# S5 token gather and scatter through a DRAM scratch, and the HGRN2 gates' affine steps on ScalarE

## The chip, the cores and the metric

The kernel runs on one core of a Trainium2 chip. The metric is the device time of one execution in microseconds; of several executions the median counts. TensorE is written PE, VectorE DVE, ScalarE ACT, GpSimd POOL, and SyncE, which issues most DMAs, SP.

## What is computed

A decoder trunk of two layers over one sequence of 512 tokens and 1024 channels, in float32. Layer 0 splits one input projection `z = h @ ev_w_in` into five parts of 512 channels. The first goes through S5, a diagonal complex state space in 32 groups of 16 channels and 64 states; the four others are query, forget gate, value and output gate of HGRN2 with four heads of 128:

```
y = gelu(s5(u));  y_a = y * sigmoid(y @ w_glu + b_glu)
forget = lb + (1 - lb) * sigmoid(f_pre)
key    = (1 - lb) * sigmoid(-f_pre)
query  = silu(q_raw)
o = chunk_gated_linear(query, key, i_raw, log(forget))
y_b = rms_norm(o, norm_g) * silu(g_raw)
x = x + gate * (concat(y_a, y_b) @ ev_w_out)
```

A SwiGLU feed-forward follows, then layer 1 (GLA mixer and feed-forward) and a last norm. Each sub-layer's shift, scale and gate (adaLN) come from `cond @ ada_w`, six pieces of 1024 columns a layer.

## The kernel before, in words

Activations lie with channels on partitions and the 512 tokens in the free dimension. Each float32 weight and activation is split in a high and a low part (`whi`, `wlo`; `hhi`, `hlo`), and a projection takes three matmuls for each pair of blocks (`proj`, L275 to L277, 128x512; `proj_tok`, L299 to L301, 128x256).

The stage that the change touches is the mixer of layer 0. Its four projections per head are named hq (query), hf (forget), hv (value) and hg (output gate). They are written in this order: S5 block 0, `hg_fq(0)`, S5 block 1, values of heads 0 and 1, `hg_fq(1)`, S5 block 2, their output gates, the cores of heads 0 and 1, S5 block 3, values of heads 2 and 3, `hg_fq(2)`, outputs of heads 0 and 1, gelu, `hg_fq(3)`, gates, the S5 gate (`s5_glu`), the cores of heads 2 and 3, and the output projection. This is not the order that runs: the Tile framework's scheduler orders the instructions of each engine from their dependences and a simulated timeline, so a change in one step moves others.

`s5_block` handles 128 channels. Its input projection lies in PSUM as uT, 128 channels by 512 tokens. It wants four tokens side by side: U has partition 32 r + c, for r the place in a group of four tokens and c a channel of 32. So 16 copies of 32x128 (L775) move a piece each across partitions and gather every fourth token. Two sets of matmuls (vps, with the weights Wn made from wnp) bring U to the states; VectorE and POOL rotate them (tiles rz..a to d), two scans of VectorE (L792) run the recurrence over 128 groups, and the matmuls yp add the direct term (Kz) and the states' output (Wd0z, Wd1z). Then 16 ScalarE copies of 32x128 bring yp back to channels by tokens (`yf`). POOL makes block q + 1's tables (B..a, B..b, W..a, W..b) in the meantime.

`hg_fq` projects, takes sigmoids on ScalarE, and does query, key K and gate lg on VectorE, the last two as affine steps (`tsv`, a tensor_scalar, L111 and L113). The core of a head takes products of K and of e (query times decay) with running totals (tot) at seven levels of distance 1, 2, 4 to 64; at each, VectorE makes the products, PE the scores (`lv`, L465) and VectorE writes them under a mask into `sc`. kht, st, S and o_h follow: transposed keys, state sums, states, and outputs. y_h is the head's normalised output, yT its transpose, dgp the first step of heads 2 and 3.

The adaLN weights come in tiles `ar`, which SP loads into two buffers a size; VectorE sums them into `acc` with the condition as scalar (`ada_run`, L202 and L204), and a piece ends in four matmuls (`fold`, L210). acc02 and fold02 are the pieces 2 and 4 of layer 0, acc03 and fold03 the piece 3. Weight loads advance this chain (`ada_steps`), which keeps program order.

Of the kernel before, what the change touches and what calls it, by code (L numbers as in the profile page):

```python
# [8 lines left out]
F32 = mybir.dt.float32  # L9
# [8 lines left out]
P = 128  # L18
# [23 lines left out]
def trunk(  # L42
# [11 lines left out]

    cp = ctx.enter_context(tc.tile_pool(name="cp", bufs=1))
    wp = ctx.enter_context(tc.tile_pool(name="wp", bufs=3))
    xp = ctx.enter_context(tc.tile_pool(name="xp", bufs=1))
    hp = ctx.enter_context(tc.tile_pool(name="hp", bufs=2))
    tp = ctx.enter_context(tc.tile_pool(name="tp", bufs=1))
# [25 lines left out]
    def act(o, i, f, **kw):  # L85
        return A.activation(out=o, in_=i, func=f, **kw)  # L86
# [19 lines left out]
    def ttv(e, o, a, b, op):  # L106
        e.tensor_tensor(out=o, in0=a, in1=b, op=op)  # L107
# [147 lines left out]
        ada_steps()  # L255
        return w

    def split(e, src, name, th, tl):
        hi = tt(f"hi_{name}", th, dtype=F32R)
        lo = tt(f"lo_{name}", tl, dtype=F32R)  # L260
        act(hi, src, AF.Copy)
        ttv(e, lo, src, hi.bitcast(F32), ALU.subtract)
        return hi, lo

    def blocks(w, cols=slice(0, P)):
# [480 lines left out]
    def s5_tables(q):  # L746
# [15 lines left out]
        tact(ph, ph, AF.Sin, scale=TWO_PI)  # L762
        return cosT, ph

    def s5_block(q, uT, mats, rot):

        rho = prm[3]
        Km, Wn, (Wr, Wi) = mats
        cosT, sinT = rot
        shp = [P, 4, P]  # L770
        U = tt(f"U{q}", "X" if q < 3 else "s", (P, 4, P))
        for j in range(4):
            for s in range(4):
                r = 3 - s
                V.tensor_copy(out=U[32 * r : 32 * r + 32, j, :], in_=uT[32 * j : 32 * j + 32, s:T:4])  # L775
        vps = []
        for i in range(2):
            ps = ps_b(f"vps{q}{i}", (P, 4, P))
# [24 lines left out]
        for j in range(4):  # L803
            PE.matmul(yp[:, j, :], lhsT=Km[:, j].rearrange("p t c -> p (t c)"), rhs=U[:, j, :], start=True, stop=False)
            PE.matmul(yp[:, j, 1:], lhsT=Wr[:, j, :], rhs=t[0][:, j, 0 : P - 1], start=False, stop=False)
            PE.matmul(yp[:, j, 1:], lhsT=Wi[:, j, :], rhs=z[0][:, j, 0 : P - 1], start=False, stop=True)
        yf = tt(f"yf{q}", "r")
        for j in range(4):
            for s in range(4):
                act(yf[32 * j : 32 * j + 32, s:T:4], yp[32 * s : 32 * s + 32, j, :], AF.Copy)  # L810
        return yf

    def s5_glu(yf):
        wg = []
        for i in range(2):
            w = wsplit(wraw(s5_w_glu[0, i * 2 * P : (i + 1) * 2 * P, :], 2, f"wg{i}", T), 2, f"wg{i}", T, V)
            wg += [tuple(z[:, k, :] for z in w) for k in range(2)]
        yr = [split(V, y, f"yr{k}", "s", "s") for k, y in enumerate(yf)]
        res = []
        for m in range(4):  # L820
            ps = mm_ps(f"glu{m}")
            proj(ps, [tuple(z[:, m * P : (m + 1) * P] for z in w) for w in wg], yr)
            y = tt(f"ys{m}", "s")
            tact(y, ps, AF.Sigmoid, bias=cols2[:, 12 + m : 13 + m])
            ttv(G, y, y, yf[m], ALU.mult)
            res.append(split(V, y, f"ys{m}", "s", "s"))
        return res

# [190 lines left out]
    def hg_fq(hd):  # L1019
        c0 = S5W + hd * P  # L1020
        hi, lo = wload(win[:, c0 : c0 + P], KT, f"hq{hd}")
        psq = mm_ps(f"hq{hd}")
        proj(psq, blocks((hi, lo)), h)
        c0 = S5W + 512 + hd * P
        hi, lo = wload(win[:, c0 : c0 + P], KT, f"hf{hd}")
        ps = (ps_a if hd < 2 else mm_ps)(f"hf{hd}")
        proj(ps, blocks((hi, lo)), h)
        Q = tt(f"hq{hd}", "t")
        K = tt(f"hk{hd}", "t")
        lg = tt(f"lg{hd}", "t")  # L1030
        tact(Q, psq, AF.Sigmoid)
        tact(lg, ps, AF.Sigmoid)
        tact(K, ps, AF.Sigmoid, scale=-1.0)
        ttv(V, Q, Q, psq, ALU.mult)
        tsv(V, K, K, oml[:, hd : hd + 1], ALU.mult)
        tsv(V, lg, lg, oml[:, hd : hd + 1], ALU.mult, lb[:, hd : hd + 1], ALU.add)
        return Q, K, lg

    def hg_v(pr):
# [216 lines left out]
```

## Time and profile before

| | us |
|---|---|
| runs | 1358.05, 1355.7, 1357.15 |
| median | 1357.15 |
| the profiled execution's own time | 1364.62 |
| its span | 1362.8 |
| start of its first output-projection matmul | 295.7 |
| PE busy | 1286.2 (94%) |
| DVE busy | 797.2 (58%) |
| ACT busy | 487.5 (36%) |
| POOL busy | 151.0 (11%) |

The span is the time from the first to the last recorded instruction of the execution, and its own time is what the device counted for it; the mean granted PE clock was 0.967 of full speed. Busy time is the union of an engine's instructions, DMA issues left out. Matmuls are pipelined: a record is longer than the pitch from one to the next, so a dense stretch is counted by starts. A bracket at the end of a timeline row gives the idle time before the instruction and what ended it.

### The profile page before, as it was taken

The page shows a single profiled execution, that of the slowest core. Times are in us where ns is not written, and L with a number is a line of the kernel's source. Part 1 is how long each engine was busy: PE and PEld are TensorE (multiplying, and loading weights), DVE is VectorE, ACT ScalarE, POOL GpSimd, SP SyncE. Part 2 cuts the span into 40 slices and gives each one's busy share as a digit, 9 for nine tenths or more (in the row PEclk, how much of TensorE's full clock was granted, in tenths as well). Part 3 has the DMA queues.
Part 4 walks back from the last instruction along what each step waited for, and adds up shares of the span by engine and source line. Part 5 has one row for each costly group of instructions (what it writes and reads, how often), then busy time and mean ns, then how long its engine had stood idle before and what let it go on. Part 6 is the DMA issues. An engine that isn't in the chain of part 4 may idle for free.

```text
span 1362.8 us, 18262 instructions
## 1 busy us (share of the span) xinstructions
PE 1286.2 (94%) x6949; PEld 1103.4 (81%) x6949; DVE 797.2 (58%) x1511; ACT 487.5 (36%) x851; POOL 151.0 (11%) x148
## 2 busy tenths in 40 slices
PE   6598899799899999999999999999899999999997
PEld 3377887778888888888889999998788888888886
DVE  4979796887865566665445446557653333333344
ACT  5253556423532322222334434432442322232232
POOL 1764451120100000000000000000100000000000
PEclk9779998889899999999999999999999999999999
DMA  8624540534067768987333232213223323433222
GB/s 293 163 63 129 150 140 16 126 94 132 18 142 188 202 174 213 214 219 198 106 106 94 65 92 63 74 49 97 62 82 104 93 74 103 117 93 93 79 86 83
DMA packets 222824, 159.69 MB, mean 117 GB/s; under 512 B 16752, under 2 KB 195248, under 8 KB 222736
## 3 DMA queue, kind: packets, MB, share of 16 engines
q1 hardware_dynamic: 221696, 157.48, 42.2%
q10 hardware_dynamic: 1040, 1.05, 0.3%
q8 instruction: 54, 0.88, 0.3%
q14 instruction: 34, 0.28, 0.1%
HBM read 156.40 MB, written 2.10 MB: 116 GB/s over the span
## 4 chain that ended last, share of the span: by engine, by line
PE 78%; DVE 12%; DMA 4%; ACT 2%; issue 2%; POOL 1%; SPq 0%; DVEq 0%; ACTq 0%
PE f L275 18%; PE f L276 18%; PE f L277 18%; DMA ar<-in_ada_w_dram 3%; PE op L276 2%; PE op L275 2%; PE op L277 2%; PE lv_g L465 2%; DVE acc L204 2%; PE gr L300 1%; PE gr L301 1%; PE gr L299 1%; PE gv L301 1%; PE gv L300 1%; PE gv L299 1%
## 5 line engine op out<-in xcount | busy, mean ns | idle before, releaser
L276 PE MATMUL f<-hlo_f,whi_f 128*128 128x512 f32 (+1 forms) x736 | 281.5, 383 | 0.2 <-DVE hlo_f L116 0.2
L275 PE MATMUL f<-hhi_f,whi_f 128*128 128x512 f32 (+1 forms) x736 | 280.9, 384 | 0.5 <-ACT hhi_f L86 0.5
L277 PE MATMUL f<-hhi_f,wlo_f 128*128 128x512 f32 (+1 forms) x736 | 280.8, 382 | 0.0
L86 ACT ACTIVATE whi_f<-raw_f 128x1024 fp32r<-128x1024 f32 x88 | 93.3, 1061 | 307.0 <-PE f L276 169.3
L107 DVE TENSOR_TENSOR wlo_f<-raw_f,whi_f 128x1024 fp32r<-128x1024 f32 x88 | 107.7, 1224 | 115.1 <-ACT whi_f L86 114.8
L276 PEld LDWEIGHTS f<-hlo_f,whi_f 128*128 128x128 f32 x736 | 140.1, 190 | 27.0 <-DVE hlo_f L116 0.8
L275 PEld LDWEIGHTS f<-hhi_f,whi_f 128*128 128x128 f32 x736 | 139.8, 191 | 27.0 <-ACT hhi_f L86 1.0
L277 PEld LDWEIGHTS f<-hhi_f,wlo_f 128*128 128x128 f32 x736 | 140.1, 191 | 26.5
L204 DVE SCALAR_TENSOR_TENSOR acc<-ar,cond,acc 128x512 f32<-128x512 f32 x154 | 120.1, 780 | 41.6 <-DMA ar<-in_ada_w_dram 40.0
L277 PE MATMUL f<-hi_g,wlo_c 128*128 128x512 f32 x312 | 121.7, 390 | 0.0
L276 PE MATMUL f<-lo_g,whi_c 128*128 128x512 f32 x312 | 121.6, 390 | 0.0
L275 PE MATMUL f<-hi_g,whi_c 128*128 128x512 f32 x312 | 121.2, 390 | 0.0
L86 ACT ACTIVATE whi_c<-raw_c 128x768 fp32r<-128x768 f32 (+1 forms) x56 | 44.9, 801 | 161.8 <-PE f L276 114.1
L107 DVE TENSOR_TENSOR g<-g,f 128x512 f32<-128x512 f32 x44 | 30.3, 688 | 109.3 <-PE f L277 109.3
L107 DVE TENSOR_TENSOR wlo_c<-raw_c,whi_c 128x768 fp32r<-128x768 f32 (+1 forms) x56 | 50.3, 898 | 57.6 <-ACT whi_c L86 57.5
L276 PEld LDWEIGHTS f<-lo_g,whi_c 128*128 128x128 f32 x312 | 58.6, 188 | 12.1
L275 PEld LDWEIGHTS f<-hi_g,whi_c 128*128 128x128 f32 x312 | 58.6, 188 | 12.1
L277 PEld LDWEIGHTS f<-hi_g,wlo_c 128*128 128x128 f32 x312 | 58.6, 188 | 12.1
L116 DVE SCALAR_TENSOR_TENSOR x<-f,mod,x 128x512 f32<-128x512 f32 (+1 forms) x36 | 24.8, 689 | 39.4 <-PE f L277 39.2
L107 POOL TENSOR_TENSOR na_m<-na_m,nsq_m 128x256 f32<-128x256 f32 x7 | 5.7, 818 | 365.3 <-DMA raw_c<-in_ffn_w_dram 337.9
L300 PE MATMUL gv<-wlo_gv,hhi_m 128*128 128x256 f32 x128 | 36.7, 287 | 0.0
L301 PE MATMUL gv<-whi_gv,hlo_m 128*128 128x256 f32 x128 | 36.6, 286 | 0.0
(667 smaller groups left out, 2677.9 us busy)
## 6 DMA issues: line engine op xcount, KB each, us to landing
raw_f<-in_ffn_w_dram SPq DMA_DIRECT2D x88, 512.0 KB, 3.8
ar<-in_ada_w_dram SPq DMA_DIRECT2D x256, 128.0 KB, 3.7
ar<-in_ada_w_dram SPq DMA_DIRECT2D x64, 256.0 KB, 5.3
raw_c<-in_ffn_w_dram SPq DMA_DIRECT2D x32, 384.0 KB, 3.5
raw_c<-in_ffn_w_dram SPq DMA_DIRECT2D x24, 320.0 KB, 3.2
raw_gv<-in_od_w_in_dram SPq DMA_DIRECT2D x8, 512.0 KB, 4.4
raw_gr<-in_od_w_in_dram SPq DMA_DIRECT2D x8, 512.0 KB, 4.0
raw_o<-in_ev_w_out_dram SPq DMA_DIRECT2D x8, 384.0 KB, 3.4
```

The lines of the kernel that those rows point to most:

```text
L86: return A.activation(out=o, in_=i, func=f, **kw)
L107: e.tensor_tensor(out=o, in0=a, in1=b, op=op)
L116: V.scalar_tensor_tensor(out=o, in0=a, scalar=s, in1=b, op0=op0, op1=op1)
L204: ins = V.scalar_tensor_tensor(out=acc, in0=w, scalar=c_, in1=acc, op0=ALU.mult, op1=ALU.add)
L275: PE.matmul(ps, lhsT=hi, rhs=ah[:, ts], start=(i == 0), stop=False)
L276: PE.matmul(ps, lhsT=hi, rhs=al[:, ts], start=False, stop=False)
L277: ins = PE.matmul(ps, lhsT=lo, rhs=ah[:, ts], start=False, stop=(i == n - 1))
L299: PE.matmul(o, lhsT=ah[:, s], rhs=hi, start=(k == 0), stop=False)
L300: PE.matmul(o, lhsT=ah[:, s], rhs=lo, start=False, stop=False)
L301: PE.matmul(o, lhsT=al[:, s], rhs=hi, start=False, stop=(k == KT - 1))
L465: PE.matmul(ps[0:nk, w, :].rearrange("p (n b) -> p n b", b=b), lhsT=K[:, w * P : w * P + nk], rhs=qv[:, w * nb : (w + 1) * nb, b:], start= ...
```

## The change

Three things are changed. A helper `quarters` writes a 256 KB tile of SBUF to a DRAM scratch with one DMA on ScalarE's queue and reads it back with four DMAs of 64 KB on GpSimd's queue, each into 32 partitions, with the partitions permuted. S5's gather of U then takes four ScalarE copies of 128x128 out of PSUM (`ud`) and one `quarters`; the way back takes one ScalarE copy of 128x512 (`yo`) and one `quarters` (`yd`), and what reads y sees it through a rearranged view. In `hg_fq` the two affine steps are ScalarE activations with scale, or scale and bias, per partition.

```diff
@@ -54,6 +54,7 @@
 
     cp = ctx.enter_context(tc.tile_pool(name="cp", bufs=1))
     wp = ctx.enter_context(tc.tile_pool(name="wp", bufs=3))
+    dp = ctx.enter_context(tc.tile_pool(name="dp", bufs=1, space=bass.MemoryType.DRAM))
     xp = ctx.enter_context(tc.tile_pool(name="xp", bufs=1))
     hp = ctx.enter_context(tc.tile_pool(name="hp", bufs=2))
     tp = ctx.enter_context(tc.tile_pool(name="tp", bufs=1))
@@ -255,11 +256,11 @@
         ada_steps()
         return w
 
-    def split(e, src, name, th, tl):
+    def split(e, src, name, th, tl, view=lambda z: z):
         hi = tt(f"hi_{name}", th, dtype=F32R)
         lo = tt(f"lo_{name}", tl, dtype=F32R)
-        act(hi, src, AF.Copy)
-        ttv(e, lo, src, hi.bitcast(F32), ALU.subtract)
+        act(view(hi), src, AF.Copy)
+        ttv(e, view(lo), src, view(hi.bitcast(F32)), ALU.subtract)
         return hi, lo
 
     def blocks(w, cols=slice(0, P)):
@@ -762,17 +763,25 @@
         tact(ph, ph, AF.Sin, scale=TWO_PI)
         return cosT, ph
 
+    def quarters(name, dst, src):
+
+        dr = dp.tile([4, P, P], F32, name=f"q_{name}", tag=f"q_{name}")
+        nc.scalar.dma_start(out=dr.rearrange("b p n -> p b n"), in_=src)
+        for b in range(4):
+            nc.gpsimd.dma_start(out=dst[32 * b : 32 * b + 32], in_=dr[b].rearrange("(a c) n -> c a n", c=32))
+
     def s5_block(q, uT, mats, rot):
 
         rho = prm[3]
         Km, Wn, (Wr, Wi) = mats
         cosT, sinT = rot
         shp = [P, 4, P]
+
+        ud = tt(f"ud{q}", "s", (P, 4, P))
+        for s in range(4):
+            act(ud[:, 3 - s, :], uT[:, s:T:4], AF.Copy)
         U = tt(f"U{q}", "X" if q < 3 else "s", (P, 4, P))
-        for j in range(4):
-            for s in range(4):
-                r = 3 - s
-                V.tensor_copy(out=U[32 * r : 32 * r + 32, j, :], in_=uT[32 * j : 32 * j + 32, s:T:4])
+        quarters(f"U{q}", U, ud)
         vps = []
         for i in range(2):
             ps = ps_b(f"vps{q}{i}", (P, 4, P))
@@ -804,25 +813,25 @@
             PE.matmul(yp[:, j, :], lhsT=Km[:, j].rearrange("p t c -> p (t c)"), rhs=U[:, j, :], start=True, stop=False)
             PE.matmul(yp[:, j, 1:], lhsT=Wr[:, j, :], rhs=t[0][:, j, 0 : P - 1], start=False, stop=False)
             PE.matmul(yp[:, j, 1:], lhsT=Wi[:, j, :], rhs=z[0][:, j, 0 : P - 1], start=False, stop=True)
-        yf = tt(f"yf{q}", "r")
-        for j in range(4):
-            for s in range(4):
-                act(yf[32 * j : 32 * j + 32, s:T:4], yp[32 * s : 32 * s + 32, j, :], AF.Copy)
-        return yf
+        yo = tt(f"yo{q}", "s", (P, 4, P))
+        act(yo, yp, AF.Copy)
+        yd = tt(f"yd{q}", "r", (P, 4, P))
+        quarters(f"y{q}", yd, yo)
+        return yd.rearrange("p s n -> p n s")
 
     def s5_glu(yf):
         wg = []
         for i in range(2):
             w = wsplit(wraw(s5_w_glu[0, i * 2 * P : (i + 1) * 2 * P, :], 2, f"wg{i}", T), 2, f"wg{i}", T, V)
             wg += [tuple(z[:, k, :] for z in w) for k in range(2)]
-        yr = [split(V, y, f"yr{k}", "s", "s") for k, y in enumerate(yf)]
+        yr = [split(V, y, f"yr{k}", "s", "s", lambda z: z.rearrange("p (n s) -> p n s", s=4)) for k, y in enumerate(yf)]
         res = []
         for m in range(4):
             ps = mm_ps(f"glu{m}")
             proj(ps, [tuple(z[:, m * P : (m + 1) * P] for z in w) for w in wg], yr)
             y = tt(f"ys{m}", "s")
             tact(y, ps, AF.Sigmoid, bias=cols2[:, 12 + m : 13 + m])
-            ttv(G, y, y, yf[m], ALU.mult)
+            ttv(G, y.rearrange("p (n s) -> p n s", s=4), y.rearrange("p (n s) -> p n s", s=4), yf[m], ALU.mult)
             res.append(split(V, y, f"ys{m}", "s", "s"))
         return res
 
@@ -1032,8 +1041,8 @@
         tact(lg, ps, AF.Sigmoid)
         tact(K, ps, AF.Sigmoid, scale=-1.0)
         ttv(V, Q, Q, psq, ALU.mult)
-        tsv(V, K, K, oml[:, hd : hd + 1], ALU.mult)
-        tsv(V, lg, lg, oml[:, hd : hd + 1], ALU.mult, lb[:, hd : hd + 1], ALU.add)
+        act(K, K, AF.Copy, scale=oml[:, hd : hd + 1])
+        act(lg, lg, AF.Identity, scale=oml[:, hd : hd + 1], bias=lb[:, hd : hd + 1])
         return Q, K, lg
 
     def hg_v(pr):
```

Since a scheduler orders the instructions, the change moves many. Three places follow. Names carry a number after the underscore that only tells buffers apart; line numbers after the change are one or more higher.

First PE's queue in the cores of heads 0 and 1 at level 8 (`lv_h08`, `lv_h18`). Before:

```order
L275 MATMUL hq2_2169<-hhi_m0_451,whi_hq2_2147 128x512
L276 MATMUL hq2_2169<-hlo_m0_452,whi_hq2_2147 128x512
L465 MATMUL lv_h08_1807<-e0_h0_1739,hk0_1072 120x64 x4
L277 MATMUL hq2_2169<-hhi_m0_451,wlo_hq2_2149 128x512
L275 MATMUL hq2_2169<-hhi_m0_451,whi_hq2_2147 128x512
L276 MATMUL hq2_2169<-hlo_m0_452,whi_hq2_2147 128x512
L277 MATMUL hq2_2169<-hhi_m0_451,wlo_hq2_2149 128x512
L275 MATMUL hf2_2206<-hhi_m0_451,whi_hf2_2196 128x512
L721 MATMUL M3_1556<-s5c_658,Bd0z_775 128x16
L465 MATMUL lv_h18_1816<-e0_h1_1758,hk1_1443 120x64 x4
```

and now, with U2 the third S5 block's gathered input and hg10 the output-gate projection of heads 2 and 3:

```order
L301 MATMUL hg10_2385<-wlo_hg11_2383,hhi_m0_453 128x256
L302 MATMUL hg10_2385<-whi_hg11_2381,hlo_m0_454 128x256
L466 MATMUL lv_h04_1752<-e0_h0_1702,hk0_1061 124x64 x4
L466 MATMUL lv_h14_1761<-e0_h1_1721,hk1_1419 124x64 x4
L789 MATMUL vps20_1439<-U2_1432,wn20_1191 128x128 x4
L789 MATMUL vps21_1444<-U2_1432,wn21_1198 128x128 x4
L466 MATMUL lv_h08_1770<-e0_h0_1702,hk0_1061 120x64 x4
L466 MATMUL lv_h18_1779<-e0_h1_1721,hk1_1419 120x64 x4
L813 MATMUL yp2_1473<-U2_1432,Kz_812 128x128
L466 MATMUL lv_h016_1788<-e0_h0_1702,hk0_1061 112x64 x4
L466 MATMUL lv_h116_1797<-e0_h1_1721,hk1_1419 112x64 x4
L466 MATMUL lv_h032_1806<-e0_h0_1702,hk0_1061 96x64 x4
```

Dense projections stood between the levels; now levels 4 to 32 stand behind hg10's last matmul, one after the other, with block 2's matmuls between them.

Second POOL's queue while it makes block 1's tables (B1, W1) and takes part in block 0's rotation (rz0). Before:

```order
L107 TENSOR_TENSOR W0a_783<-W0a_783 128x256
L107 TENSOR_TENSOR W0b_784<-W0b_784 128x256
L107 TENSOR_TENSOR B1a_920<-s5b0_648,s5L_239 128x256
L107 TENSOR_TENSOR B1a_920<-s5b1_653,s5L_239 128x256
...
L107 TENSOR_TENSOR W1a_932<-s5c_658,s5L_239 128x256 x2
...
L107 TENSOR_TENSOR B1a_920<-B1a_920 128x256
L107 TENSOR_TENSOR B1b_921<-B1b_921 128x256
L107 TENSOR_TENSOR W1a_932<-W1a_932 128x256
L107 TENSOR_TENSOR rz0c_868<-rz0c_868,rz0d_869 128x512
```

and now:

```order
L108 TENSOR_TENSOR W0b_786<-W0b_786 128x256
L771 DMA U0_846<-q_U0_847 32x4x128 x4
L108 TENSOR_TENSOR rz0c_865<-rz0c_865,rz0d_866 128x512
...
L108 TENSOR_TENSOR B1a_909<-s5b0_650,s5L_241 128x256
...
L108 TENSOR_TENSOR W1a_921<-s5c_660,s5L_241 128x256 x2
...
L108 TENSOR_TENSOR B1a_909<-B1a_909 128x256
L108 TENSOR_TENSOR B1b_910<-B1b_910 128x256
L771 DMA yd0_902<-q_y0_903 32x4x128 x4
...
L108 TENSOR_TENSOR W1b_922<-W1b_922 128x256
L771 DMA U1_1075<-q_U1_1076 32x4x128 x4
```

Block 1's tables stood ahead of rz0; now they stand behind the four loads of U0 and rz0, the last products of W1 behind the loads of yd0, and U1's loads behind those.

Third PE's queue at the start of the S5 gate (glu0 to glu3) and at fold03. Before:

```order
L511 MATMUL o_h10_1921<-S_1911,e0_h1_1758 128x128
L275 MATMUL glu0_2567<-hi_yr0_2551,whi_wg0_2541 128x512
L276 MATMUL glu0_2567<-lo_yr0_2552,whi_wg0_2541 128x512
...
L277 MATMUL glu3_2627<-hi_yr3_2563,wlo_wg1_2549 128x512
L210 MATMUL fold03_2423<-ind2_121,acc03_2164 128x2 x4
L451 MATMUL dgp_h3_2667<-hq3_2390,hk3_2391 128x128 x2
```

and now, from the second-last group of the stage, block 3's (vps3, yp3):

```order
L789 MATMUL vps30_1904<-U3_1897,wn30_1548 128x128 x4
L789 MATMUL vps31_1909<-U3_1897,wn31_1555 128x128 x4
L813 MATMUL yp3_1938<-U3_1897,Kz_812 128x128
L211 MATMUL fold02_2106<-ind4_124,acc02_982 128x4 x4
L814 MATMUL yp3_1938<-rz3a_1914,Wd0z_793 128x127
...
L815 MATMUL yp3_1938<-rz3b_1915,Wd1z_795 128x127
L452 MATMUL dgp_h2_2598<-hq2_2181,hk2_2182 128x128 x4
L466 MATMUL lv_h21_2607<-e0_h2_2603,hk2_2182 127x64 x4
L211 MATMUL fold03_2373<-ind2_123,acc03_2114 128x2 x4
L276 MATMUL glu0_2517<-hi_yr0_2501,whi_wg0_2491 128x512
```

The gate began right behind the heads' outputs, with fold03 behind all of it; now block 3's matmuls, fold02, head 2's first products and fold03 are ahead of the gate's first matmul.

## Rows read from the trace of the kernel before

**Rows 1.** The page's first line: span and instructions of the profiled execution.

```profile
span 1362.8 us, 18262 instructions
```

**Rows 2.** Stretch, length, busy of PE, PEld, DVE, ACT, POOL (instructions), PEclk, DMA share, GB/s.

```profile
94.00:195.00 101.00, 88.63 (x614) 82.69 (x612) 90.03 (x167) 46.90 (x105) 42.04 (x31) 0.95 0.51 141
...
251.00:268.80 17.80, 14.07 (x82) 13.69 (x82) 12.27 (x24) 11.31 (x29) 0.00 (x0) 0.71 0.64 153
271.60:295.70 24.10, 21.60 (x94) 18.39 (x95) 22.61 (x60) 9.28 (x22) 8.72 (x6) 0.79 0.53 134
296.00:345.00 49.00, 48.36 (x290) 41.12 (x289) 36.35 (x76) 13.73 (x31) 0.21 (x1) 1.00 0.34 102
345.00:1363.00 1018.00, 997.80 (x5312) 861.17 (x5310) 522.71 (x931) 332.47 (x528) 27.10 (x29) 0.99 0.42 113
```

**Rows 3.** The chain of waits in 94 to 296 us, summed by line.

```profile
by line: DMA ar<-in_ada_w_dram 12.7%; DVE acc L204 10.4%; issue 8.7%; DVE U L775 5.5%; POOL rz0c L107 3.6%; DVE e_h L107 3.4%; ACT yf L86 2.9%; SPq L188 2.6%; DVE wlo_hq L107 2.1%; DVE tot_h L107 2.0%; PE lv_h L465 2.0%; DVE sc_h L479 1.8%;
```

**Rows 4.** One line's or tile's instructions: ns min/median/max, first and last start (us).

```profile
L775 DVE COPY U<-u x64: 271/286/298, 89.8 to 236.3; 32x128 f32<-32x128 f32 x64
...
L86 ACT ACTIVATE yf<-yp x64: 382/391/403, 139.7 to 265.1; 32x128 f32<-32x128 f32 x64
...
L86 ACT ACTIVATE lg<-hf x4: 579/586/592, 110.3 to 269.6; 128x512 f32<-128x512 f32 x4
L113 DVE TENSOR_SCALAR lg<-lg,lbm x4: 528/540/548, 117.6 to 272.3; 128x512 f32<-128x512 f32 x4
```

**Rows 5.** DMAs by kind (KB each, median us to landing), and issues from the timeline.

```profile
ar<-in_ada_w_dram SPq DMA_DIRECT2D x64, 256.0 KB, 5.3
...
out_dram<-ob ACTq DMA_DIRECT2D x2, 256.0 KB, 2.8
...
254.47 3.30 SPq L188 DMA_DIRECT2D ar<-in_ada_w_dram  x4
...
278.45 0.33 ACTq L1134 DMA_DIRECT2D ng<-in_gla_norm_g_dram  x1
```

**Rows 6.** Timeline of POOL: start us, us, engine, line, operation; idle before and releaser.

```profile
115.31 7.25 POOL L107 TENSOR_TENSOR rz0c<-rz0c,rz0d 128x512 f32<-128x512 f32 x1 [24.73 <-DVE rz0d L107]
...
247.63 1.29 POOL L107 TENSOR_TENSOR rz3c<-rz3d,ph 128x512 f32<-128x512 f32 x1 [3.98 <-DVE rz3d L792]
```

**Rows 7.** Timeline of PE in dense projections, 98 and 109 us.

```profile
98.20 0.39 PE L277 MATMUL hq<-hhi_m,wlo_hq 128*128 128x512 f32 x1
98.43 0.39 PE L275 MATMUL hq<-hhi_m,whi_hq 128*128 128x512 f32 x1
...
109.60 0.28 PE L301 MATMUL hv<-whi_hv,hlo_m 128*128 128x256 f32 x1
109.72 0.28 PE L299 MATMUL hv<-whi_hv,hhi_m 128*128 128x256 f32 x1
```

**Rows 8.** Timeline, four marks: head 0's level 4, acc03's first sum, S5 gate, fold03.

```profile
191.11 1.76 PE L465 MATMUL lv_h<-e_h,hk 128*124 128x64 f32 x8
...
251.84 0.47 DVE L202 TENSOR_SCALAR acc<-ar,cond 128x512 f32<-128x512 f32 x1
...
271.59 0.60 PE L275 MATMUL glu<-hi_yr,whi_wg 128*128 128x512 f32 x1 [2.79 <-DVE hq L107]
...
284.19 0.95 PE L210 MATMUL fold<-ind,acc 128*128 128x2 f32 x8
```

**Rows 9.** Timeline of VectorE at 189 and 251 us, and a scan in the chain.

```profile
188.88 0.41 DVE L107 TENSOR_TENSOR hk<-hk,tot_h 128x256 f32<-128x256 f32 x1
...
189.55 0.71 DVE L479 COPY_PREDICATED sc_h<-msk,lv_h 126x256 f32<-126x256 uint8 x1
190.07 0.72 DVE L204 SCALAR_TENSOR_TENSOR acc<-ar,cond,acc 128x512 f32<-128x512 f32 x1
...
251.16 0.68 DVE L107 TENSOR_TENSOR rz3a<-rz3b,cos 128x512 f32<-128x512 f32 x1
...
247.49 3.37 DVE rz3b L792 x4
```

## Prediction

> **What bounds the kernel now.** I read the profile from the outside in. The execution that the rows come from spans 1362.8 us [rows 1]; its own time is 1364.62 us, 7.5 above the median of the three runs shown (1357.15), so I sum changes on the profile and add the result to the median. Next, busy time by stretch [rows 2]. From 345 us to the end TensorE is busy 997.8 of 1018 us, and in 296:345, where the first layer's output projection starts, 48.36 of 49. No work of the diff lies there, and the changed order is the same there in practice. So all is decided before the first output-projection matmul, which in this execution is at 295.7, and every us by which that moves is a us of the whole. The stretches of the first mixer are another matter. In 94:195 VectorE is busy 90.03 of 101 us, TensorE 88.63. In 251:268.8, the tail of HGRN2 heads 0 and 1, TensorE is busy 14.07 of 17.8 at a granted clock of 0.71. The chain of waits over 94:296 [rows 3] names no single owner: the adaLN weight tiles (DMA ar 12.7%, VectorE's sums on them 10.4%), the very copies that the change takes away (U at L775 5.5%, yf 2.9%), and a spread of vector work. So three clocks run side by side here: TensorE's dense projections, VectorE's mix of S5 and HGRN2 work, and the adaLN chain, which the S5 gate's matmuls wait for by order or by PSUM slots. The question is how the change reorders them.
>
> **What goes and what comes.** VectorE loses 64 copies of 0.286 us (18.3) and 8 affine steps of at most 0.540 (4.3) [rows 4]. ScalarE loses 64 copies of 0.391 (25.0) and gains 16 copies of 128x128, 4 of 128x512 and 8 affine steps; at 0.59, the price of its 128x512 form, the latter twelve cost 7.1 [rows 4]. That is a gain on both engines, and if order stayed it would be a gain in time. In exchange each of eight gathers is a chain: ScalarE issues one store of 256 KB, GpSimd issues four loads of 64 KB, and U or yd is there only when the last has landed. The nearest rows: a store of 256 KB from ScalarE's queue lands in 2.8, its issue is 0.33, SP's issues go at 3.30 for four, 0.83 each [rows 5]. No DMA is issued by GpSimd in the trace of before. I bound one such issue by 0.33 from below and by 7.25 from above, the time that GpSimd's rz0c took in a stretch where VectorE was busy nine tenths, against 1.29 for the same form on block 3 [rows 6]. I take 0.83, the other queue that issues four in a row, and 2.8 for a 64 KB landing, the one row for a small transfer on a compute engine's queue. So a gather is 0.33 + 2.8 + 4 x 0.83 + 2.8 = 9.3 us, against 16 x 0.286 = 4.6 for U's copies and 16 x 0.391 = 6.3 for y's. By length alone the change loses 4.7 + 3.0 a block where nothing covers it.
>
> **What the order does with it.** This is the larger part, and it is read from the order, with durations from the rows.
>
> Step 1, dense work pulled ahead. Before, heads 0 and 1 run their seven levels in among the projections of hv1, hq2, hf2 and hq3. After, no dense matmul is between the end of hg10 and the start of hg12. Ahead of the first level-4 matmul of head 0 there are now 192 matmuls of hq and hf and 336 of hv and hg, where there were 96 and 275 (u's 96 are ahead in both). At 0.23 a 128x512 (98.20 to 98.43) and 0.12 a 128x256 [rows 7] that is 44.2 + 40.3 = 84.5 us against 22.1 + 33.0 = 55.1, so 29.4 more; eight block-2 matmuls (vps2, under 0.23 each) move behind, so +27.6. Head 0's level 4 stood at 191.1 [rows 8]. What comes back: in 94:195 TensorE was idle 12.4 us, and VectorE there sheds 48 x 0.286 + 4 x 0.540 = 15.9. I take 4 of the 12.4, with 0 and 12 as ends, because GpSimd's queue has new waits in the same stretch: block 1's table products now stand behind U0's loads, and U1's loads behind yd0's. Level 4 comes at 191.1 + 27.6 - 4 = **215**.
>
> Step 2, the levels with nothing beside them. What remains is a chain on VectorE: levels 8, 16 and 32 of two heads, a triple of products and masked copy at 1.19 each (188.88 to 190.07), level 64's four products at 0.41, and S5 block 2's nine rotation products at 0.68 and two scans of 3.37 [rows 9]: 7.1 + 1.6 + 6.1 + 6.7 = 21.5. Before, all of that lay under dense matmuls. That gives **236.5**.
>
> Step 3, head states and outputs, in the same order as before: the stretch that held them was 17.8 [rows 2]. **254.3**.
>
> Step 4, block 3's gather with nothing over it. ud3 stands on ScalarE behind wn31, the Kz and Wd1z pieces, head 1's squares and a gelu, 15 instructions at about 0.39, 5.9. Then the gather, 9.3. hg12's 48 matmuls (5.8) are the only work beside it. vps3 comes at 254.3 + 15.2 = **269.5**. In the kernel before it was done under the dense matmuls.
>
> Step 5, the adaLN chain. The S5 gate's first matmul needs a slot of PSUM; after the change it also stands behind fold03 on TensorE. acc03 starts only behind block 3's rotations on VectorE: six products at 0.68 and two scans at 3.37, 10.8, so at 280.3. It goes through eight tiles with two buffers, so three rounds of landing 5.3 [rows 5], issue 0.83 and two sums of 0.72 [rows 9], 7.6 each, then two tiles more of sums, 2.9: 25.6. Before, the same chain took 32.4, from 251.84 to 284.19 [rows 8], with fold03 behind the whole gate; 32.4 is the upper end. fold03 at 306 and the gate's first matmul right after, against 271.6 before [rows 8]: **+34**. The other way in, y3's return, comes to 269.5 + 6.1 + 6.7 + 2.8 for block 3's matmuls, then 0.6 + 9.3 for copy and gather and 2.5 for gelu, sigmoid, product: 297.5, so the adaLN chain decides, by 8.
>
> Step 6, what comes back behind the gate. Between its start and the output projection lay 24.1 us [rows 2], of which 48 matmuls at 0.23 need 11; the rest was head outputs, transposes and head 2's first products, which now stand ahead of it. I take 6 off, with 0 and 13 as ends. Net **+28**: 1392.6 for the profiled execution, **1385** for the median.
>
> The affine steps alone cost nothing: ScalarE is busy 46.9 of 101 us [rows 2], and lg is used behind e, products and sums that VectorE must do in any case; without that cover heads 2 and 3 would each pay 2 x 0.59.
>
> **A rule that speaks against the change.** The rows show GpSimd's 128x512 product at 7.25 and at 1.29 [rows 6], the long one where VectorE hardly rests. The Trainium skill, page "SBUF — State Buffer", section "SBUF: two separate sides", says that GpSimd writes the descriptors of the DMAs that it issues and is kept from doing so while VectorE holds the port pair they share; it advises issuing from another queue. The trace agrees as far as GpSimd's arithmetic goes; of its DMAs no row here shows anything. By this rule alone the sum would be that of the first rival; by the rows it stays at +28.
>
> **The rivals.**
> *GpSimd's issues are held up too* (0.16). Were an issue to take 7.25 in place of 0.83, each such loss would add 6.4. One lost issue in each of the two gathers that nothing covers (U2 or U3, and y3) gives +13, **1398** (0.11). All four in both, 8 x 6.4 = 51, give **1436** (0.05). For it: 94:195. Against: TensorE's tail has VectorE waiting too, 12.27 busy of 17.8 [rows 2].
> *The order costs nothing and the engines' relief counts* (0.15): faster. The mechanism is VectorE in 94:195: if it is what paces TensorE there, its 15.9 us come back up to TensorE's idle 12.4, and dense work pulled ahead is only work not done later, so that the levels' exposed chain is met by a shorter stretch before the output projection. That needs the gathers to lie hidden and acc03 to start early. It decides if level 4 comes before 203 and fold03 before 272. Price -12.4, **1345**; up to 18.3 + 4.3 = 22.6 at the end. Against it: with the projections gone from under the levels, steps 2 to 4 have 52 us with 6 of dense matmuls.
> *No change* (0.05): the pulled-ahead work and the exposed chain balance, 1357. That the change does nothing is excluded, as the order differs throughout this stage.
>
> **How the numbers follow.** The forecast, +28, has 0.64. Its own ends: y3 decides in place of the adaLN chain (-8), 8 more us recovered in step 1, 7 more in step 6, together +5; upward 32.4 for the chain (+7), nothing recovered in step 1 (+4) or in step 6 (+6), together +45. These are not all likely at once. The range goes from 1355 to 1410: it takes in the forecast's ends but its very top, one lost issue a gather and no change, and leaves out most of the faster case and the worst hold-up, some 0.18. Measurements of this kernel tell 0.2%, 2.7 us, from no change. Faster: 0.15. Same: 0.05. Slower: 0.64 + 0.16 = 0.80.
>
> **What would show it.** Right: level 4 of head 0 near 215, vps3 near 270, the gate's first matmul near 306; TensorE idle between hg10's end and hg12; the sums of acc03 behind rz3; every stretch after the output projection's start as long as before. Step 1 is wrong if level 4 comes by 203; step 4 if U3's loads land within 5 us of its store; step 5 if the gate waits for y3's product or starts before 290. The whole is wrong if the projections that went ahead shorten the later stretch by as much as they delay the levels.

## The result, and the profile after

| | before | changed |
|---|---|---|
| runs, us | 1358.05, 1355.7, 1357.15, 1362.3 | 1407.81, 1403.18, 1407.38, 1399.88 |
| median, us | 1357.6 | 1405.28 |
| ratio, 95% interval | | 1.0341 [1.0298, 1.0384] |
| profiled execution: time, span | 1364.62, 1362.8 | 1407.81, 1406.0 |

The change makes the kernel slower by 47.7 us between medians. The two profiled executions lie 43.2 apart, because that of before was 7 above its median and that of the changed kernel 2.5 above; traces are compared by 43.2.

The page of the changed kernel: busy time of the engines, and GpSimd's DMA queue (q0: packets, MB, share of 16 engines):

```profile
PE 1292.2 (92%) x6949; PEld 1108.6 (79%) x6949; DVE 781.7 (56%) x1439; ACT 477.0 (34%) x815; POOL 152.1 (11%) x180
...
q0 software_dynamic: 1024, 2.10, 0.5%
```

GpSimd's queue is new, 1024 packets and 2.10 MB; ScalarE's grew from 1040 packets to 5264. TensorE's busy time is 6 us longer (same 6949 matmuls, 1286.2 before), VectorE's 15.5 shorter (797.2). Relief on VectorE is there; the span still grew.

Where it grew, from the windows (stretch, length, busy of PE, PEld, DVE, ACT, POOL, PEclk, DMA share, GB/s), cut where the output projection runs dense. First the kernel before, then the changed one:

```profile
94.00:295.70 201.70, 175.01 (x1109) 159.27 (x1108) 170.54 (x341) 95.84 (x214) 70.39 (x45) 0.91 0.43 116
295.70:1363.00 1067.30, 1046.46 (x5602) 902.59 (x5601) 559.06 (x1007) 346.50 (x557) 27.61 (x30) 0.99 0.41 112
```

```profile
94.00:338.90 244.90, 179.61 (x1108) 162.72 (x1107) 154.77 (x280) 83.50 (x175) 77.38 (x87) 0.83 0.42 107
338.90:1406.00 1067.10, 1046.76 (x5592) 903.32 (x5591) 558.81 (x1005) 348.22 (x559) 29.75 (x31) 0.99 0.41 113
```

All 43.2 us lie between 94 us and the dense output projection: 244.9 long in place of 201.7. Behind that the changed kernel takes 1067.1 and the kernel before 1067.3, so nothing is lost or given back there. In that stretch TensorE is busy 179.6 against 175.0, so it idles 65.3 us where it idled 26.7. The cost is 38.6 us of idle TensorE, plus 4.6 by which as many matmuls (1108 and 1109) are busy longer. The granted clock is lower there, 0.83 against 0.91, in a stretch in which TensorE is busy 73% against 87%. VectorE is busy 155 of 245 us (before 171 of 202): it was relieved and then stood still.

One correction to what stands ahead: the 295.7 called there the first matmul of the output projection is where it runs dense. Single ones, between transposes and head 2's levels, stand from 286.45:

```profile
286.45 0.47 PE L275 MATMUL op<-hi_ys,whi_o 128*128 128x512 f32 x1
```

In the changed kernel the first is at 338.88 and they run dense from there. The sums are not touched, since they take dense to dense.

The stage in steps, from the same view of the changed kernel, cut at the marks that the prediction named:

```profile
94.00:228.50 134.50, 112.73 (x717) 102.87 (x717) 79.36 (x118) 51.37 (x104) 44.37 (x52) 0.91 0.55 141
228.50:256.70 28.20, 18.39 (x122) 17.03 (x120) 23.78 (x49) 0.97 (x2) 13.30 (x14) 0.70 0.02 7
256.70:267.40 10.70, 9.13 (x71) 7.96 (x70) 4.79 (x21) 4.84 (x17) 3.60 (x6) 1.00 0.17 51
267.40:281.50 14.10, 8.59 (x59) 8.11 (x58) 6.26 (x30) 9.06 (x29) 2.17 (x4) 0.76 0.12 38
281.50:322.60 41.10, 14.47 (x74) 13.10 (x73) 31.01 (x50) 12.56 (x17) 6.79 (x7) 0.61 0.50 127
322.60:338.90 16.30, 16.30 (x74) 13.65 (x74) 9.58 (x18) 4.69 (x7) 7.14 (x5) 0.83 0.22 48
```

and the marks themselves, from TensorE's timeline (the bracket is the idle time ahead and what ended it):

```profile
116.59 1.62 PE L789 MATMUL vps<-U,wn 128*128 128x128 f32 x6 [9.52 <-DMA U<-q_U]
...
176.40 0.98 PE L789 MATMUL vps<-U,wn 128*128 128x128 f32 x3 [4.26 <-DMA U<-q_U]
...
228.53 0.65 PE L466 MATMUL lv_h<-e_h,hk 128*124 128x64 f32 x5
...
256.71 0.55 PE L490 MATMUL kht_h<-cs,hk 128*128 128x128 f32 x3
...
281.54 1.73 PE L789 MATMUL vps<-U,wn 128*128 128x128 f32 x14
...
320.95 1.84 PE L211 MATMUL fold<-ind,acc 128*128 128x2 f32 x8 [1.33 <-DVE acc L205]
322.65 0.77 PE L276 MATMUL glu<-hi_yr,whi_wg 128*128 128x512 f32 x1
...
338.88 0.48 PE L276 MATMUL op<-hi_ys,whi_o 128*128 128x512 f32 x1
```

In 256.7:267.4 the head outputs run at a clock of 1.00 and TensorE is nearly full; in 281.5:322.6, block 3 and the adaLN chain, it is busy 14.5 of 41.1 at 0.61. fold03 is at 320.95, the gate's first matmul at 322.65, where fold03 was at 284.19 and the gate at 271.59 [rows 8]: the two have changed places, as the order showed. The first and the second gather are waited for by TensorE, 9.52 and 4.26 us, the third 1.09; the fourth is not. Over the whole stage (what TensorE waited for, us in total, times, longest):

```profile
PE vps L789 <- DMA U<-q_U: 14.9, 3, 9.5
```

So 14.9 of TensorE's 65.3 idle us end with a gather's landing; most of the rest ends with VectorE.

### The profile page after: what moved, and what is told of

Same layout as the page of the kernel before. It is cut to its first block, busy times and chain, and to the rows that moved or that the text cites. A ratio compares the mean times of both kernels' runs of the same rounds, so it can differ in the third digit from the quotient of the medians.

```text
span 1406.0 us, 18241 instructions
## 1 busy us (share of the span) xinstructions
PE 1292.2 (92%) x6949; PEld 1108.6 (79%) x6949; DVE 781.7 (56%) x1439; ACT 477.0 (34%) x815; POOL 152.1 (11%) x180
## 3 DMA queue, kind: packets, MB, share of 16 engines
q0 software_dynamic: 1024, 2.10, 0.5%
## 4 chain that ended last, share of the span: by engine, by line
PE 81%; DVE 7%; DMA 6%; ACT 3%; issue 2%; SPq 0%; POOL 0%; DVEq 0%; ACTq 0%; POOLq 0%
PE f L276 17%; PE f L277 17%; PE f L278 17%; DMA ar<-in_ada_w_dram 4%; PE op L277 2%; PE op L276 2%; PE op L278 2%; PE lv_g L466 2%; PE gr L301 1%; PE gr L302 1%; PE gr L300 1%; PE gv L302 1%; PE gv L301 1%; PE gv L300 1%; PE lv_h L466 1%
## 5 line engine op out<-in xcount | busy, mean ns | idle before, releaser
L277 PEld LDWEIGHTS f<-hlo_f,whi_f 128*128 128x128 f32 x736 | 139.7, 190 | 26.7 <-DVE hlo_f L117 0.6
L205 DVE SCALAR_TENSOR_TENSOR acc<-ar,cond,acc 128x512 f32<-128x512 f32 x154 | 116.3, 756 | 44.0 <-DMA ar<-in_ada_w_dram 42.0
L466 PE MATMUL lv_h<-e_h,hk 128*127 128x64 f32 (+6 forms) x224 | 28.4, 281 | 11.8 <-DVE sc_h L480 8.7
L466 PEld LDWEIGHTS lv_h<-e_h,hk 128*127 128x127 f32 (+6 forms) x224 | 27.2, 198 | 14.2 <-issue 10.0
```

The lines of the kernel that those rows point to most:

```text
L205: ins = V.scalar_tensor_tensor(out=acc, in0=w, scalar=c_, in1=acc, op0=ALU.mult, op1=ALU.add)
L277: PE.matmul(ps, lhsT=hi, rhs=al[:, ts], start=False, stop=False)
L466: PE.matmul(ps[0:nk, w, :].rearrange("p (n b) -> p n b", b=b), lhsT=K[:, w * P : w * P + nk], rhs=qv[:, w * nb : (w + 1) * nb, b:], start= ...
```

## The experiments

Each run's ratio is to runs of the kernel before on the same chip. Theory A: the loss lies in the order of the instructions. B: in the gathers' round trips. C: in GpSimd's issues being held up. D: in the affine steps on ScalarE.

**1. The affine steps alone.** The kernel before with

```diff
-        tsv(V, K, K, oml[:, hd : hd + 1], ALU.mult)
-        tsv(V, lg, lg, oml[:, hd : hd + 1], ALU.mult, lb[:, hd : hd + 1], ALU.add)
+        act(K, K, AF.Copy, scale=oml[:, hd : hd + 1])
+        act(lg, lg, AF.Identity, scale=oml[:, hd : hd + 1], bias=lb[:, hd : hd + 1])
```

> The kernel before with only the HGRN2 affine steps moved to ScalarE; S5's copies stay. Theory A (the loss lies in the order: dense matmuls pulled ahead of the levels, so that levels and gathers lie bare): 335 dense matmuls stand ahead of head 0's level 4, 371 before, 528 with the whole change, so the time stays near before, 1353 to 1362. Theory B (the loss is the gathers' round trips, 9 us each where nothing covers them): no gather here, so the same. Rival D (the affine steps lengthen ScalarE's queue, and the levels wait for it): slower by over 5, 1362 or more.

Measured 1356.58 against 1359.66, ratio 0.9979 [0.9962, 0.9996]. In this order D falls: this third of the change costs nothing, and by the interval it is a gain of up to 0.4%.

**2. Both DMA ways without the affine steps.** The changed kernel with these four lines the other way round.

> The changed kernel with the affine steps back on VectorE; both DMA ways stay. Its order is as the changed kernel's (528 dense matmuls ahead of level 4). Theories A and B: within 6 of the changed kernel, 1399 to 1411. Rival D: lower than 1399.

Measured 1397.6, ratio 1.0279 [1.0259, 1.0299]. That is 1.4 below the range of theories A and B, and in the range of rival D. By the medians the affine steps cost 7.7 us where the order is the changed one, though the intervals of the two ratios still overlap by a hair. In TensorE's timeline level 4 comes at 222.02 (228.53 in the changed kernel) and the gate at 314.89 (322.65):

```profile
314.89 0.77 PE L276 MATMUL glu<-hi_yr,whi_wg 128*128 128x512 f32 x1
```

So D is not wholly out: in the changed order the affine steps seem to cost some 8 us, while they cost nothing in run 1. Why there and not here was not tried. The bulk, 38 us, is the DMA ways'.

**3. Other buffers for the two staging tiles.** The changed kernel with

```diff
-        ud = tt(f"ud{q}", "s", (P, 4, P))
+        ud = tt(f"ud{q}", "n", (P, 4, P))
-        yo = tt(f"yo{q}", "s", (P, 4, P))
+        yo = tt(f"yo{q}", "r", (P, 4, P))
```

The tag names the pool of equal buffers that a tile is taken from: s has 16, n 4, r 8 (`SLOTS`). Nothing that is computed or transferred changes.

> The changed kernel, all eight gathers and the affine steps as they are; only the two staging tiles take other buffers, ud the tag n and yo the tag r in place of s. The scheduler then puts 341 dense matmuls ahead of level 4 (371 before, 528 changed). Theory A: the loss goes with the order, 1350 to 1372. Theory B: the round trips are all still there, over 1385. Rival C (GpSimd's issues and tables held up): also over 1385.

Measured 1367.69, ratio 1.0064 [1.0041, 1.0086]. Of 47.7 us, some 38 are gone (by the ratios 1.0341 and 1.0064), with all eight gathers and all 32 GpSimd loads in place. B and C, which expected the loss whatever the order, fall; what the gathers cost inside the changed order is another question, and there TensorE waits 14.9 us for them. Its marks on TensorE (level 4 of head 0, block 3's first matmuls, the gate):

```profile
190.07 0.97 PE L466 MATMUL lv_h<-e_h,hk 128*124 128x64 f32 x8
...
236.66 0.83 PE L789 MATMUL vps<-U,wn 128*128 128x128 f32 x6
...
282.90 0.77 PE L276 MATMUL glu<-hi_yr,whi_wg 128*128 128x512 f32 x1
```

Level 4 is at 190.07, as before (191.11 [rows 8]), and vps3 at 236.66, where in the kernel before its first matmuls start at 232.94 and its last ten at 236.66. TensorE waits for no gather in this stage. Only the gate is late, 282.90 against 271.59 [rows 8].

**4. The order without the change.** The kernel before with its own copies and no DMA, TensorE's and VectorE's instructions chained in the changed kernel's order; ScalarE, GpSimd and SyncE, and the copies and affine steps on VectorE, as the scheduler puts them around that:

```diff
         trunk(tc, *args)
+        pin(tc)
```

`pin` adds an order-only edge from each instruction to the next of a list, for the 6397 of TensorE and 1439 of VectorE that both kernels share.

> The kernel before with its own copies and affine steps and no gather by DMA, TensorE's and VectorE's instructions held in the changed kernel's order (the copies and affine steps where the scheduler puts them). Theory A: most of the loss appears without any DMA, 1385 to 1405. Theory B: 1355 to 1368.

Measured 1429.04, ratio 1.0514 [1.0495, 1.0533]. That is 24 above A's range; what makes it so much was not tried (the old copies stand inside the chained order here). In its windows TensorE is busy 118 of 146 us up to level 4 and 16 of 45 in the adaLN chain:

```profile
94.00:240.50 146.50, 118.39 (x719) 107.24 (x719) 94.45 (x165) 56.93 (x118) 31.19 (x31) 0.86 0.43 117
...
300.00:345.20 45.20, 15.80 (x85) 14.32 (x83) 31.79 (x52) 15.10 (x31) 4.66 (x3) 0.62 0.42 105
```

The order, with no gather in it and with the old copies fitted in, costs 69 us. From vps3 (301.12) to the gate (345.15) it takes 44.0, against 41.1 in the changed kernel, and TensorE waits there for the same things, here in this run and then in the changed kernel:

```profile
PE dgp_h L451 <- DVE lo_y_h L107: 13.9, 1, 13.9
PE yp L805 <- DVE rz3a L107: 8.4, 1, 8.4
```

```profile
PE dgp_h L452 <- DVE lo_y_h L108: 11.3, 1, 11.3
PE yp L814 <- DVE rz3a L108: 8.4, 1, 8.4
```

B falls as the main cause. How the 47.7 us divide cannot be had from this run, since it loses more than the change does.

**5. The change in the order of before.** As run 3, with TensorE and VectorE chained in the order of the kernel before.

> The changed kernel with its eight gathers and ScalarE affine steps, staging tiles in the tags n and r, and TensorE's and VectorE's instructions held in the order of the kernel before (ScalarE, GpSimd and SyncE as the scheduler puts them). Theory A (order is the whole loss): 1350 to 1362, the 8 us that the run with other buffers kept above before are gone. Theory B' (what is left are round trips that lie bare whatever the order): 1364 to 1380, with TensorE waiting for U's loads and the gate for y3's.

Measured 1361.99, ratio 1.0031 [1.0017, 1.0044]: at A's upper end and below what B' expected. TensorE waits for a load of U once in this run, for 0.47 us:

```profile
232.57 0.46 PE L789 MATMUL vps<-U,wn 128*128 128x128 f32 x2 [0.47 <-DMA U<-q_U]
```

What stands out is y3's way back, in ScalarE's timeline, on GpSimd's and on TensorE's:

```profile
255.73 0.60 ACT L87 ACTIVATE yo<-yp 128x512 f32<-128x512 f32 x1 [2.01 <-PE yp L815]
256.36 0.37 ACTq L769 DMA_DIRECT2D q_y<-yo  x1
...
261.63 2.19 POOL L771 DMA_DIRECT2D yd<-q_y  x4 [13.33 <-DMA q_y<-yo]
...
269.03 1.10 ACT L87 ACTIVATE yd<-yd 128x512 f32<-128x512 f32 x1 [1.81 <-DMA yd<-q_y]
...
273.08 0.80 PE L276 MATMUL glu<-hi_yr,whi_wg 128*128 128x512 f32 x1 [7.04 <-ACT hk L87]
```

yo is copied at 255.73, its store issued at 256.36; GpSimd starts its four loads at 261.63; the gelu on yd starts at 269.03 having waited for the loads, 13.3 us after the copy began, where the old copies were 16 of 0.391, 6.3 [rows 4]. The sigmoids stand behind that gelu, and the gate's first matmul behind hk's sigmoid, after 7.04 us of idle. So a round trip delays the gate at the one place where nothing covers it; run 12 tries what that is worth. One thing stays open: this run has the staging tiles in n and r, so what waiting for a buffer of the tag s would cost in the order of before was not tried.

**6 and 7. One half each.** With the affine steps on ScalarE and the staging tile out of s: U by DMA and y by the old copies,

> U by DMA (staging tile in tag n), y by the old ScalarE copies, affine steps on ScalarE. If the 8 us left in the run with other buffers come from y's way back: 1352 to 1361, no slower than the kernel with the affine steps alone by over 4. If they come from U's gathers: 1364 to 1374.

and U by the old copies and y by DMA:

> The other half: U by the old VectorE copies, y by DMA (staging tile in tag r), affine steps on ScalarE. If the 8 us left come from y's way back: 1364 to 1374. If from U's gathers: 1352 to 1361.

Measured 1363.13, 1.0039 [1.0024, 1.0053], and 1362.57, 1.0027 [1.0012, 1.0042]. Both fall between the two ranges that were to tell them apart. Against the kernel before, the halves cost 5.3 and 3.7 us by the ratios, and run 3, which has both, 8.7: each has a share. The scheduler orders each of these kernels anew, so a share is that of a half together with its order.

**8. Gathers one block early.** As run 3, with the gather taken out of the block and written ahead of it:

```diff
+    Us = [s5_gather(q, ups[q]) for q in range(2)]
...
+        if len(Us) < 4 and len(Us) == q + 1:
+            Us.append(s5_gather(len(Us), ups[len(Us)]))
-        yfs.append(s5_block(q, ups[q], mats[q], rot[q]))
+        yfs.append(s5_block(q, Us[q], mats[q], rot[q]))
```

> All gathers by DMA with staging tiles in n and r, and each block's gather written one block earlier (blocks 0 and 1 ahead of block 0). If U's round trips still cost something in the run with other buffers, 4 to 9 us less than that run's 1367.7, 1358 to 1364; if what is left lies at y's end, 1364 to 1371, for there fold03 stands ahead of the gate again, as in the changed kernel.

Measured 1355.55, ratio 0.9968 [0.9947, 0.9989]: 2.5 us below the range expected if U's round trips still cost something. Writing the gathers early is worth some 12 us against run 3, and the kernel is now no slower than before (by the interval 0.1 to 0.5% faster). That it is U's round trips that cost them in run 3 is not shown: TensorE waits for no load of U there either, and the order is another one.

**9 and 10. One staging tile at a time.** The changed kernel with only ud in n, and with only yo in r:

> The changed kernel with only ud's buffer moved to the tag n; yo stays in s. The scheduler puts 384 dense matmuls ahead of head 0's level 4 (341 with both moved, 528 in the changed kernel), and all 576 still ahead of block 3's first matmul. Theory A (the time follows the order): between the two, 1374 to 1392. If one staging tile alone made the loss: under 1370 or over 1398.

> The changed kernel with only yo's buffer moved to the tag r; ud stays in s. 434 dense matmuls ahead of level 4, 576 ahead of block 3. Theory A: between the two and over the run with ud alone moved, 1380 to 1400.

Measured 1369.67, 1.0080 [1.0053, 1.0107], and 1370.19, 1.0090 [1.0065, 1.0115]. Both misses: the time does not follow the number of dense matmuls ahead of level 4 (384 and 434, against 341 and 528). Moving either tile removes some 35 of 47.7 us. It takes both in s to make the loss, and the count was the wrong measure. (Run 9 lies by 0.3 us in the range of "one staging tile alone", but run 10 removes as much.) Level 4 and the gate in TensorE's timelines, of run 9 and then of run 10:

```profile
191.81 0.98 PE L466 MATMUL lv_h<-e_h,hk 128*124 128x64 f32 x8
...
287.52 0.80 PE L276 MATMUL glu<-hi_yr,whi_wg 128*128 128x512 f32 x1 [0.21 <-ACT hk L87]
```

```profile
200.30 1.84 PE L466 MATMUL lv_h<-e_h,hk 128*124 128x64 f32 x16
...
285.42 0.78 PE L276 MATMUL glu<-hi_yr,whi_wg 128*128 128x512 f32 x1
```

Level 4 is 2 and 10 us behind run 3's, and the gate is within 5 of it. In runs 3, 9 and 10 the gate starts ahead of fold03 (286.64, 300.86 and 291.18), in the changed kernel behind it. That this decides is not shown: in run 8 fold03 (276.98) stands ahead of the gate (279.18) too, and nothing is lost.

**11. Another queue for the loads.** The changed kernel with TensorE and VectorE held in its order, and

```diff
-            nc.gpsimd.dma_start(out=dst[32 * b : 32 * b + 32], in_=dr[b].rearrange("(a c) n -> c a n", c=32))
+            nc.sync.dma_start(out=dst[32 * b : 32 * b + 32], in_=dr[b].rearrange("(a c) n -> c a n", c=32))
```

> The changed kernel with the gathers' 32 loads issued by SyncE in place of GpSimd; TensorE and VectorE held in the changed kernel's order, so that only the queue differs. Rival C (GpSimd's issues are held up by VectorE): faster than the changed kernel by over 6, under 1399. Otherwise 1399 to 1415, the upper part if SyncE's weight loads stand behind the stores.

Measured 1400.6, ratio 1.0309 [1.0284, 1.0335]: inside the range without C, 4.7 below the changed kernel by the medians, with overlapping intervals. The kinds of DMA in the trace, issuing queue, KB each and median us to landing, of this run and of the changed kernel:

```profile
U<-q_U SPq DMA_DIRECT2D x16, 64.0 KB, 1.9
yd<-q_y SPq DMA_DIRECT2D x16, 64.0 KB, 2.1
```

```profile
q_U<-ud ACTq DMA_DIRECT2D x4, 256.0 KB, 3.6
U<-q_U POOLq DMA_DIRECT2D x16, 64.0 KB, 2.8
```

A load of 64 KB lands in 2.8 from GpSimd's queue and in 1.9 to 2.1 from SyncE's. The issues of U's loads (ns min/median/max, first and last start in us) in this run and in the changed kernel:

```profile
L771 SPq DMA_DIRECT2D U<-q_U x16: 303/430/437, 107.9 to 268.5; - x16
```

```profile
L771 POOL DMA_DIRECT2D U<-q_U x16: 548/551/712, 109.6 to 278.3; - x16
```

GpSimd's and VectorE's timelines in the changed kernel have the first four issues, beside one VectorE product that runs through them:

```profile
109.57 2.34 POOL L771 DMA_DIRECT2D U<-q_U  x4 [28.44 <-DMA q_U<-ud]
...
109.71 1.22 DVE L108 TENSOR_TENSOR wlo_hv<-raw_hv,whi_hv 128x1024 fp32r<-128x1024 f32 x1
```

Four issues take 2.34 us there, with wlo_hv (two inputs in SBUF) running from 109.71 to 110.93, and 2.17 at 276.72, where VectorE has only small operations. No issue of U's loads took over 0.712. C falls: beside the operations that VectorE ran here, GpSimd's issues were not held up. The queue is not free, though. With SyncE's shorter issues and landings TensorE's waits for U fall from 14.9 to 5.8 us:

```profile
PE vps L789 <- DMA U<-q_U: 5.8, 3, 4.6
```

**12. Early gathers, and the last block's y by copies.** As run 8, with `yo` and `quarters` for blocks 0 to 2 and the sixteen old copies for block 3.

> Gathers by DMA one block early, staging tiles in n and r, y by DMA for blocks 0 to 2 and by the old copies for block 3, affine steps on ScalarE. If what is left in the run with early gathers is y3's way back ahead of the S5 gate: 3 to 8 us less than its 1355.6, 1347 to 1353. If the gate waits for fold03 anyway: 1353 to 1360.

Measured 1350.74, ratio 0.9947 [0.9929, 0.9966]: 4.8 below run 8 by the medians (the intervals overlap), in the range expected if y3's way back was left. The gate starts at 265.50 us and fold03 follows behind:

```profile
265.50 0.40 PE L276 MATMUL glu<-hi_yr,whi_wg 128*128 128x512 f32 x1
...
266.99 1.05 PE L211 MATMUL fold<-ind,acc 128*128 128x2 f32 x8 [0.16 <-DVE acc L205]
```

By the medians this is 7.4 us faster than before, and some 54 faster than the changed kernel.

## Why the prediction was right, and its sum too small

The direction, the place and the main mechanism held: slower, with everything lost between 94 us and the output projection, and in the order of TensorE and VectorE more than in the added DMAs' length alone. Of what was to show it, TensorE's idle time behind hg10, fold03 ahead of the gate and an unchanged rest are in the trace above, and acc03's first sum stands among rz3's last products; the marks are later than named (level 4 at 228.5 for 215, vps3 at 281.5 for 270, the gate at 322.65 for 306). The measured 1405.28 lies in the range, near its top, 20 above the forecast. It is also 2.7 above the top of the forecast's own ends (+45, where the medians differ by 47.7; the two profiles, 43.2 apart, are inside). No term of the sum reaches the range's 1410, so that the range held is in part luck. By the forecast's own steps, on the profiled execution (1392.6 forecast, 1407.81 measured):

| step | forecast | measured | difference |
|---|---|---|---|
| 1, level 4 at | 215 | 228.5 | +13.5 |
| 2, levels and block 2 | 21.5 | 28.2 | +6.7 |
| 3, states and outputs | 17.8 | 10.7 | -7.1 |
| 4, block 3's gather | 15.2 | 14.1 | -1.1 |
| 5, vps3 to the gate | 36.5 | 41.1 | +4.6 |
| 6, gate to output projection, against 24.1 | -6 | -7.9 | -1.9 |

They add to 14.7 of 15.2, the rest is rounding.

**Step 1** is the mis-sized term. It counted 29.4 us more dense work ahead of level 4, 27.6 net, rightly (TensorE is busy 112.7 there against 84.7 in 94:191.1 before), and then gave 4 back because VectorE sheds 15.9 us there. Nothing came back, and 9.4 more were lost. Up to level 4 TensorE was idle 21.8 of 134.5 us, where it had been idle 12.4 of the 97.1 before, although VectorE was down to 79 of 134.5. Its waits there, in TensorE's view:

```profile
PE vps L789 <- DMA U<-q_U: 13.8, 2, 9.5
PE yp L814 <- DVE rz0a L108: 5.6, 1, 5.6
```

The first two gathers, 13.8 us, and the rotation behind the first gather, 5.6. The prediction priced a bare gather at 9.3 and charged one in step 4, but in step 1 U0's and U1's enter only as a reason to take 4 us back and not 12; as waits of TensorE they stand at nothing. Dense work was there, but it stood behind vps0 and vps1 in TensorE's queue and started only after them. (The first store, too, left at 105.30, four us behind the last ud copy, from ScalarE's queue.) An upper end of one bare gather each for U0 and U1 would have held the 9.52 and 4.26 that were measured.

**Step 2** was 6.7 longer, and not as summed. Its two scans took 1.36 and 1.34, not 3.37 each: the 3.37 of [rows 9] is a scan of before that ran beside two GpSimd products (247.63 to 250.26), while the other scan of that block took 1.36. Against that VectorE stood idle 4.4 of the 28.2 us, there were two masked copies and two products more than counted, and many products were longer. Beside block 2's rotation on GpSimd, VectorE's products of 0.68 and 0.41 [rows 9] took 1.75 and 1.48:

```profile
235.56 1.30 POOL L108 TENSOR_TENSOR rz2c<-rz2c,rz2d 128x512 f32<-128x512 f32 x1 [6.90 <-DVE rz2d L108]
...
235.66 1.75 DVE L108 TENSOR_TENSOR rz2a<-rz2a,rz2b 128x512 f32<-128x512 f32 x1
...
243.48 1.59 POOL L108 TENSOR_TENSOR rz2d<-rz2d,cos 128x512 f32<-128x512 f32 x1
...
243.87 1.48 DVE L108 TENSOR_TENSOR hk<-hk,tot_h 128x256 f32<-128x256 f32 x1
```

VectorE's product starts 0.10 behind GpSimd's of 1.30 and ends 0.55 behind its end. The Trainium skill, page "SBUF — State Buffer", section "SBUF: two separate sides", says that where a VectorE operation with two SBUF inputs meets a GpSimd operation that reads SBUF, the one that starts first holds the shared port pair for its whole length. The trace agrees here. The prediction drew on the same section for the opposite direction, GpSimd's DMA descriptors kept waiting by VectorE; of that the changed kernel, with 0.55 us an issue and 0.712 at most (run 11), shows nothing.

**Step 3** was too long by 7.1: by the timeline of before, block 3's last matmuls and part of the projection hg12 lay in that stretch, and now they lie elsewhere. **Step 4** is right to 1 us, with the kinds' medians near the terms: store 3.6 against 2.8, four issues 2.2 against 3.3, landing 2.8 against 2.8. But it did not lie bare: TensorE waited 3.98 us for ud ahead of hg12, and hg12's 48 matmuls, 7.7 us long at a lower clock (0.76 in this step) where 5.8 were counted, ran up to vps3, which waited for no load. **Step 5**: the adaLN chain did decide, as said. acc03 began at 292.00, in VectorE's timeline:

```profile
292.00 0.47 DVE L203 TENSOR_SCALAR acc<-ar,cond 128x512 f32<-128x512 f32 x1
```

That is 10.5 behind vps3 (forecast 10.8, in part by luck: the two scans took 3.7 for 6.7, and other work stood between them), and it took 29.0 to fold03 (forecast 25.6, bound 32.4). **Step 6** was inside its ends. Two slips do not move the sum: steps 2 to 4 add to 54.5 us, not the 52 of the faster rival, and the upper end +45 is 1402, inside the range and not left out of it.

The rivals: the held-up issues fell (runs 3 and 11). The faster one, that order costs nothing and the engines' relief counts, named a gain that the change as it stands does not have; with the buffers moved, the gathers early and block 3's y by copies the kernel is 7.4 us faster than before (run 12). How much of that is the engines' relief and how much the new order was not tried. The affine steps, which the prediction put at nothing, may have cost some 8 us in the changed order (run 2). What no step of the prediction saw is why the order changed. It argued from the order as given. Runs 3, 9 and 10 show that the buffers of the two staging tiles decide it: with both in s the scheduler makes the bad order, with either out of s a nearly good one. By which of its rules the scheduler comes from the one to the other was not tried.

## What to carry to other kernels

Where a scheduler sets the order, a new tile's buffer is part of the change: look at the order of the engines that wait, and try another pool for the tile before judging the operation that uses it. A round trip through DRAM costs what the engine that needs it waits: TensorE waited 14.9 us for U's loads in the changed order and not at all in runs 3 and 8, while the last block's y, 13.3 us from its copy to its use in run 5, stood ahead of the gate. VectorE was busy nine tenths of 94:195 before [rows 2], and its relief was worth nothing in the changed kernel, where TensorE waited in order for something else.

## What the runs showed of the hardware that was not expected

A DMA of 64 KB issued by GpSimd took 0.55 us to issue, where the same DMA issued by SyncE took 0.43 (run 11). It landed in 2.8 in the changed kernel, where SyncE's landed in 1.9 to 2.1; but the landing moved with the kernel, and U's loads from GpSimd's queue took a median of 6.9 in run 3, 6.5 in run 5 and 6.3 in run 8. VectorE's two-input products, running through an issue, did not lengthen it much (2.34 for four, against 2.17). VectorE's 128x512 product went from 0.68 to 1.75 beside one of GpSimd.
